# Moving a per-column scale past the down product, and summing seven block products inside three PSUM banks, in the feed-forward part of a hybrid encoder layer

## The chip, the core and the metric

The kernel runs on one core of a Trainium2 chip. Its time is the device time of one execution in microseconds (us). The core has TensorE (PE in the profile; PEld is its weight load), VectorE (DVE), ScalarE (ACT), GpSimd (POOL) and SyncE (SP), which here issues nearly all DMAs. The five engines run side by side and meet through semaphores. Matrix products end in PSUM, eight banks of 128 x 512 f32 values.

## The reference

One encoder layer for 1024 prompt positions and 32 new ones (T = 1056 columns), D = 1024, feed-forward width 4096. Two attention branches come first. What matters here is the last function:

```
h = x + m @ w_out
u = rmsnorm(h, g_ffn) @ w_up
y = h + square(relu(u)) @ w_down
```

The rmsnorm multiplies each position by r = 1/sqrt(mean(h^2) + eps). Everything is f32. As r is positive and belongs to a position, relu(r u)^2 = r^2 relu(u)^2, and r^2 can be applied after the down product too.

## The kernel before, in words

**Split products.** All matrices lie transposed: 128 features on the partitions, positions along the free dimension. An f32 operand is split into a high part and a rest (`xh`, `xl`; `wh`, `wl`), and each 128 x 128 block costs three matmuls in one PSUM chain (`three`): high by high, high by rest, rest by high. A weight unit is 128 x 512 values: a DMA into `wst` (three buffers), a cast on ACT to `wh`, a subtraction on POOL to `wl` (`unit`, `split`). `wh` and `wl` have WB = 5 buffers each, so a buffer is free again when the block that used it five units earlier has ended.

**Two groups.** Positions 0 to 511 are group one (one chunk of 512 columns), 512 to 1055 group two (two chunks of 272). In group one the feed-forward part is interleaved with the later half of attention until that ends. `go_up(f)` makes one of 32 blocks of 128 features of u (24 matmuls), `go_down(e, q)` adds to output block e of y the part of the down product that comes from up blocks 4q to 4q + 3 (12 matmuls a chunk; e and q run over 0 to 7). Group one goes up one block ahead: U0, then for each q four U and eight D (for q = 6 six D, the other two, `KEEP`, after the last three U). It has two PSUM banks, tag `pj`, for both kinds of block.

**Group two** makes two up blocks at once, for both chunks, with seven products of half the depth in place of eight (`go_up_quad`). A product is 12 matmuls of 272 columns, so a quad is 84 matmuls, and there are 16 quads. `quad_units` makes the operands on the weight side: four additions, two `sl` subtractions on DVE, two on POOL, three `wl` subtractions on POOL. On the data side they are made once, in `quarters`. Each product has a bank of its own (six banks `pj`); DVE adds them together through SBUF tiles (`part`), seven additions a quad. The down blocks use two other banks (`pd`).

**The scale.** `ffn_group` begins with a ones matmul that sums `g.acc` over the partitions, and `rsqrt` (DVE, a Sqrt on ACT, DVE). Its result `rb2` is read by every `done` of an up block: relu times r on DVE (`ru` from `pj`), square on POOL (`ru` from `ru`), cast on ACT (`xh` from `ru`), rest on DVE (`xl` from `ru`, `xh`). `go_down`'s `done` adds the bank to y, which holds h, on DVE.

**What sets the order.** Every instruction is first recorded by `Plan`, with its dependencies, a rank and a number in program order. `Plan.run` then lays out each engine's queue: whenever an engine is free in its model of durations, it takes, of the instructions that are ready, the one with the lowest (rank, number). Ranks are FAST 0 (evacuation of PSUM), PREP 1 (weights), MAIN 2 (attention), FILL 3 (the products here). The model puts some 300 ns after each instruction before another engine may use its result. The order is then fixed; on the chip each queue runs in it and waits on semaphores. As `issue` calls all of them, every row of the profile has line L408; groups are told apart by tiles.

Of the kernel before, what the change touches and what calls it, by code (L numbers as in the profile page):

```python
# [9 lines left out]
F32 = mybir.dt.float32  # L10
# [406 lines left out]
class Layer:  # L417
# [47 lines left out]
    def three(self, ps, wh, wl, xh, xl, first, last):  # L465

        mm = self.nc.tensor.matmul
        mm(ps, wh, xh, start=first, stop=False)
        mm(ps, wh, xl, start=False, stop=False)
        mm(ps, wl, xh, start=False, stop=last)  # L470
# [24 lines left out]
    def run(self):  # L495
# [32 lines left out]
        self.dg = dt([16, 128, T], "dg")  # L528

# [790 lines left out]
    def out(self, g):  # L1320

        nc, a = self.nc, self.a
        for e in (0, 4, 1, 5, 2, 6, 3, 7) if g.i else range(KB):
            units = [self.unit(a["w_out"][e, j]) for j in range(2)]

            def done(c, cs, ps, e=e):
# [4 lines left out]
                nc.vector.tensor_add(hv, ps, xr)  # L1331
                if g.i:
                    self.quarters(g, e, c, hv)
# [80 lines left out]

    def ffn_group(self, g, late=iter(())):
        nc, a, i = self.nc, self.a, g.i
        rb2 = g.acc
        for c, cs in enumerate(g.chunks):
            ps = self.bank("pj")
            nc.tensor.matmul(ps[:, :g.n], self.ones, g.acc[c], start=True, stop=True)  # L1420
            with nc.rank(FAST):
                self.rsqrt(rb2[c], ps[:, :g.n], D, lambda n: g.tmp(n, "pb", 3))
        nq, us = DFF // 512, {}

        def go_up(f):
            units = [self.unit(a["w_up"][f, j]) for j in range(2)]
            us[f] = uh, ul = g.mh[:, f % 8], g.ml[:, f % 8]

            def done(c, cs, ps):
                r = g.tmp("ru", "pb", 3)  # L1430
                nc.vector.scalar_tensor_tensor(r, ps, 0.0, rb2[c], op0=ALU.max, op1=ALU.mult)
                nc.gpsimd.tensor_mul(r, r, r)
                nc.scalar.copy(uh[:, cs], r)
                nc.vector.tensor_sub(ul[:, cs], r, uh.bitcast(F32)[:, cs])

            self.column_block(units, lambda k, cs: (g.h[:, k, cs], g.l[:, k, cs]), done, g.chunks)

        def go_up_quad(f):

            a11, a12, a22, s1, s2, s3, s4 = self.quad_units(f)  # L1440
            for i in range(2):
                us[f + i] = g.mh[:, (f + i) % 8], g.ml[:, (f + i) % 8]
            n = g.n
            ta, tb, tc, td = ([(th[:, k], tl[:, k]) for k in range(4)] for th, tl in g.sums)
            x = lambda j, c: [(g.h[:, 4 * j + k, c * n:c * n + n], g.l[:, 4 * j + k, c * n:c * n + n]) for k in range(4)]

            def product(w, xs):
                ps = self.bank("pj")[:, :n]
                with nc.rank(FILL):
                    for k in range(4):  # L1450
                        ks = slice(k * 128, k * 128 + 128)
                        self.three(ps, w[0][:, ks], w[1][:, ks], *xs[k], k == 0, k == 3)
                return ps

            z = [nc.tile(self.op, [128, 2, n], F32, "part", tag="o32", bufs=4) for _ in range(2)]
            p1, u2, u3, u4 = z[0][:, 0], z[0][:, 1], z[1][:, 0], z[1][:, 1]
            add = nc.vector.tensor_add

            def done(i, c, ps):
                cs = slice(c * n, c * n + n)  # L1460
                uh, ul = us[f + i]
                r = g.tmp("ru", "pb", 3)
                nc.vector.scalar_tensor_tensor(r, ps, 0.0, rb2[c], op0=ALU.max, op1=ALU.mult)
                nc.gpsimd.tensor_mul(r, r, r)
                nc.scalar.copy(uh[:, cs], r)
                nc.vector.tensor_sub(ul[:, cs], r, uh.bitcast(F32)[:, cs])

            ps = product(a11, x(0, 0))
            with nc.rank(FAST):
                nc.scalar.copy(p1, ps)  # L1470
            p5 = product(s1, ta)
            ps = product(s2, tb)
            with nc.rank(FAST):
                add(u2, ps, p1)
                add(u4, p5, u2)
            ps = product(a12, x(1, 0))
            with nc.rank(FAST):
                add(ps, ps, p1)
                done(0, 0, ps)
            ps = product(s3, tc)  # L1480
            with nc.rank(FAST):
                add(u3, ps, u2)
                add(ps, ps, u4)
                done(1, 1, ps)
            ps = product(s4, x(1, 1))
            with nc.rank(FAST):
                add(ps, ps, u4)
                done(0, 1, ps)
            ps = product(a22, td)
            with nc.rank(FAST):  # L1490
                add(ps, ps, u3)
                done(1, 0, ps)

        def go_down(e, q):
            units = [self.unit(a["w_down"][e, q])]

            def done(c, cs, ps):
                nc.vector.tensor_add(g.y[:, e, cs], ps, g.y[:, e, cs])
                if q == nq - 1:
                    nc.sync.dma_start(self.o["yT"][:, e, slice(g.lo + cs.start, g.lo + cs.stop)], g.y[:, e, cs])  # L1500

            self.column_block(units, lambda k, cs: (us[4 * q + k][0][:, cs], us[4 * q + k][1][:, cs]), done, g.chunks,
                              kn=4, tag="pd" if g.i else "pj")

# [13 lines left out]
        if g.i:  # L1518
            go_up_quad(0)
            go_up_quad(2)  # L1520
# [7 lines left out]
        go_up(0)  # L1528
        for q in range(nq):
# [91 lines left out]
```

## Time and profile before

| | |
|---|---|
| median of 3 runs (lowest, highest) | 1769.09 us (1766.96, 1771.07) |
| span of the profiled execution | 1767.0 us |
| time of the profiled execution outside its span | not listed |
| PE, PEld, DVE, ACT, POOL busy share | 98%, 91%, 67%, 53%, 60% |
| group one's feed-forward part | about 843 to 1296 us, attention beside it until about 1124 |
| group two's branch and output projection | about 1296 to 1391 us |
| group two's feed-forward part | 1391 us to the end |

The profile names an engine, an operation, "out<-in" by tile names, shapes, a count, then busy time and mean duration, then the engine's idle time before these instructions and what ended it. A matmul's busy time overlaps the next one's, so the pace of PE is read from starts, not from durations. In a timeline row the figures are start, duration, instruction, and in brackets the idle time before it with its releaser. In a windows row each engine has its busy time and, in brackets, its number of instructions, then the granted clock, the DMA share and GB/s.

### The profile page before, as it was taken

What the parts mean: (1) busy time and instruction counts of PE and PEld (TensorE: products, weight loads), DVE (VectorE), ACT (ScalarE), POOL (GpSimd) and SP (SyncE); (2) the same over time, 40 slices, a digit from 0 to 9 for tenths busy, and PEclk for the clock granted to TensorE, in tenths of its full rate; (3) what the DMA queues carried; (4) which work ended last, traced back from release to release, by engine and by line L of the source; (5) the groups of instructions that cost most, each with busy time, mean ns of one, the idle gap of its engine ahead of it and who ended that gap; (6) DMA issues with size and microseconds to landing.
All of it is one profiled execution on the core that took longest, in us unless ns stands there. A gap on an engine that the chain in (4) does not pass through costs nothing.

```text
span 1767.0 us, 32459 instructions
## 1 busy us (share of the span) xinstructions
PE 1739.5 (98%) x11394; PEld 1600.1 (91%) x11394; DVE 1175.5 (67%) x2427; ACT 932.7 (53%) x2007; POOL 1054.6 (60%) x901
## 2 busy tenths in 40 slices
PE   8999999999999999999999999999999999999999
PEld 7999999999899888888888888888899999999999
DVE  7555678999666645788975556333357897777764
ACT  7444598973255676766655545432236543333331
POOL 3623232435366574899875555675558986666663
PEclk9999999999999999999999999999999999999999
DMA  8244451544566668555254353433374333333312
GB/s 258 72 133 118 116 177 59 148 144 143 178 179 168 169 183 225 175 163 151 69 162 123 118 154 98 144 109 99 106 237 137 95 104 92 94 91 96 96 48 88
DMA packets 152851, 234.90 MB, mean 133 GB/s; under 512 B 27248, under 2 KB 54480, under 8 KB 152688
## 3 DMA queue, kind: packets, MB, share of 16 engines
q1 hardware_dynamic: 152256, 232.48, 45.8%
q8 instruction: 90, 1.47, 0.4%
q14 instruction: 73, 0.60, 0.1%
q10 hardware_dynamic: 432, 0.34, 0.1%
HBM read 182.58 MB, written 50.08 MB: 132 GB/s over the span
## 4 chain that ended last, share of the span: by engine, by line
PE 85%; DVE 6%; DMA 4%; POOL 3%; issue 1%; ACT 1%; SPq 0%; ACTq 0%; POOLq 0%; DVEq 0%
PE pj L408 53%; PE s L408 13%; PE pd L408 10%; PE t L408 4%; PE o L408 4%; DMA q<-dq 1%; POOL wl L408 1%; DVE xl L408 1%; DMA k<-dk 1%; DVE raw L408 1%; DVE acc L408 1%; DVE rw L408 0%; DMA o<-do 0%; SPq L408 0%; POOL acc L408 0%
## 5 line engine op out<-in xcount | busy, mean ns | idle before, releaser
L408 POOL TENSOR_TENSOR wl<-wst,wh 128x512 fp32r<-128x512 f32 x350 | 488.5, 1400 | 388.4 <-ACT wh L408 358.2
L408 PE MATMUL pj<-xh,wh 128*128 128x512 f32 (+1 forms) x1600 | 557.3, 348 | 0.6 <-DVE vt L408 0.3
L408 PE MATMUL pj<-xh,wl 128*128 128x512 f32 (+1 forms) x1600 | 557.4, 349 | 0.0
L408 PE MATMUL pj<-xl,wh 128*128 128x512 f32 (+1 forms) x1600 | 555.8, 348 | 0.0
L408 ACT CAST wh<-wst 128x512 fp32r<-128x512 f32 x350 | 216.8, 621 | 361.7 <-PE pj L408 222.0
L408 PEld LDWEIGHTS pj<-xh,wh 128*128 128x128 f32 x1600 | 301.1, 188 | 33.6 <-ACT xh L408 0.7
L408 PEld LDWEIGHTS pj<-xh,wl 128*128 128x128 f32 x1600 | 300.8, 188 | 32.7
L408 PEld LDWEIGHTS pj<-xl,wh 128*128 128x128 f32 x1600 | 301.0, 188 | 32.1
L408 PE MATMUL pd<-xh,wh 128*128 128x272 f32 x512 | 147.6, 288 | 2.0 <-DVE y L408 2.0
L408 PE MATMUL pd<-xl,wh 128*128 128x272 f32 x512 | 147.7, 288 | 0.0
L408 PE MATMUL pd<-xh,wl 128*128 128x272 f32 x512 | 147.6, 288 | 0.0
L408 DVE TENSOR_TENSOR xl<-ru,xh 128x272 fp32r<-128x272 f32 (+1 forms) x96 | 114.2, 1202 | 46.0 <-ACT xh L408 45.7
L408 DVE TENSOR_TENSOR tt<-t,tt 128x512 fp32r<-128x512 f32 (+2 forms) x168 | 100.2, 622 | 40.3 <-ACT tt L408 38.6
L408 DVE TENSOR_TENSOR_SCAN rem<-rem 128x896 f32<-128x896 f32 (+6 forms) x66 | 118.7, 1823 | 10.0 <-ACT rem L408 9.8
L408 POOL TENSOR_TENSOR p<-p,rem 128x895 f32<-128x895 f32 (+6 forms) x66 | 103.3, 1578 | 29.8 <-DVE rem L408 26.4
L408 ACT ACTIVATE junk<-score,cand 128x384 bf16<-128x384 f32 (+1 forms) x124 | 116.1, 936 | 9.3 <-DVE cand L408 7.0
L408 ACT CAST tt<-t 128x512 fp32r<-128x512 f32 (+2 forms) x168 | 84.8, 540 | 48.2 <-PE t L408 42.8
L408 DVE TENSOR_TENSOR y<-pj,y 128x512 f32<-128x512 f32 x72 | 49.6, 689 | 83.9 <-PE pj L408 83.8
L408 PE MATMUL s<-k,q 128*128 128x384 f32 (+5 forms) x384 | 95.7, 356 | 7.1 <-DMA k<-dk 2.5
L408 PE MATMUL s<-wl,xh 128*128 128x256 f32 (+1 forms) x360 | 101.8, 285 | 0.2 <-POOL wl L408 0.2
L408 PEld LDWEIGHTS o<-tt,v 128*128 128x128 f32 x640 | 93.0, 189 | 9.7 <-DVE tt L408 1.1
L408 PE MATMUL s<-wh,xh 128*128 128x256 f32 (+1 forms) x360 | 100.3, 286 | 0.9 <-DVE small L408 0.7
(245 smaller groups left out, 3963.6 us busy)
## 6 DMA issues: line engine op xcount, KB each, us to landing
wst<-w_down SPq DMA_DIRECT2D x128, 256.0 KB, 2.7
q<-dq SPq DMA_DIRECT2D x64, 256.0 KB, 5.2
wst<-w_up SPq DMA_DIRECT2D x64, 256.0 KB, 2.7
raw<-w_up SPq DMA_DIRECT2D x64, 256.0 KB, 2.8
k<-dk SPq DMA_DIRECT2D x48, 256.0 KB, 3.5
v<-dv SPq DMA_DIRECT2D x48, 256.0 KB, 3.7
wst<-w_g SPq DMA_DIRECT2D x42, 256.0 KB, 3.4
dv<-vs SPq DMA_DIRECT2D x32, 256.0 KB, 2.4
```

The costliest lines, as they stand in the source:

```text
L408: fn(*args, **kw)
```

## The change

- `rsqrt` in `ffn_group` goes; `scales` computes r^2 = 1/(mean + eps) with two DVE instructions, and is called after the first up block (group one) or the first quad (group two).
- An up block is evacuated by `square`: relu on ACT (PSUM to SBUF), r by PSUM on DVE back into PSUM, cast on ACT, rest on DVE. POOL and the scale have no part in it.
- `go_up_quad`'s products lie in chains: bank px takes a11, then s2, s3 and a22 on top; pz takes s1, then s4; py takes a12. The sums in between are copied out by ACT (`keep`), and DVE adds three times a quad instead of seven. The order of the products is a11, s1, s2, s4, a12, s3, a22.
- y no longer starts as h. For q = 0 ACT copies the bank into y; later DVE adds. Block h is stored to DRAM (`dh`) in `out` and loaded again (`hx`) once y holds q = 0 to 6; POOL then makes y r^2 + h. The last q multiplies its bank by r^2 and adds it to y, both on DVE.

```diff
         nc.vector.tensor_scalar(w, w, -0.5, 1.5, op0=ALU.mult, op1=ALU.add)
         nc.vector.tensor_mul(out, out, w)
 
-    def three(self, ps, wh, wl, xh, xl, first, last):
+    def three(self, ps, wh, wl, xh, xl, first, last, **kw):
 
         mm = self.nc.tensor.matmul
-        mm(ps, wh, xh, start=first, stop=False)
-        mm(ps, wh, xl, start=False, stop=False)
-        mm(ps, wl, xh, start=False, stop=last)
+        mm(ps, wh, xh, start=first, stop=False, **kw)
+        mm(ps, wh, xl, start=False, stop=False, **kw)
+        mm(ps, wl, xh, start=False, stop=last, **kw)
 
     def column_block(self, units, rhs, done, chunks, kn=KB, tag="pj"):
 
...
         self.dv = dt([2 * H, 128, NT, 128], "dv")
         self.do = dt([2 * H, HD, T], "do")
         self.dg = dt([16, 128, T], "dg")
+        self.dh = dt([KB, 128, T], "dh")
 
         self.wpool = nc.open("w")
         xp = nc.open("x")
...
                     nc.sync.dma_start(xr, a["xT"][:, e, slice(g.lo + cs.start, g.lo + cs.stop)])
                 hv = g.y[:, e, cs]
                 nc.vector.tensor_add(hv, ps, xr)
+                nc.sync.dma_start(self.dh[e, :, slice(g.lo + cs.start, g.lo + cs.stop)], hv)
                 if g.i:
                     self.quarters(g, e, c, hv)
                 if not g.i or c == 0 or e >= 4:
...
             p22 = part(a22, self.wpool, "w", WB, G)
         return p11, p12, p22, s1, s2, s3, s4
 
+    def square(self, g, ps, uh, ul):
+
+        nc = self.nc
+        r = g.tmp("ru", "pb", 3)
+        nc.scalar.activation(r, ps, AF.Relu)
+        nc.vector.tensor_mul(ps, ps, r)
+        nc.scalar.copy(uh, ps)
+        nc.vector.tensor_sub(ul, ps, uh.bitcast(F32))
+
     def ffn_group(self, g, late=iter(())):
         nc, a, i = self.nc, self.a, g.i
+        n = g.n
         rb2 = g.acc
-        for c, cs in enumerate(g.chunks):
-            ps = self.bank("pj")
-            nc.tensor.matmul(ps[:, :g.n], self.ones, g.acc[c], start=True, stop=True)
-            with nc.rank(FAST):
-                self.rsqrt(rb2[c], ps[:, :g.n], D, lambda n: g.tmp(n, "pb", 3))
+
+        def scales():
+
+            for c in range(len(g.chunks)):
+                ps = self.bank("pj")
+                nc.tensor.matmul(ps[:, :n], self.ones, g.acc[c], start=True, stop=True)
+                with nc.rank(FAST):
+                    v = g.tmp("rv", "pb", 3)
+                    nc.vector.tensor_scalar(v, ps[:, :n], 1.0 / D, EPS, op0=ALU.mult, op1=ALU.add)
+                    nc.vector.reciprocal(rb2[c], v)
+
         nq, us = DFF // 512, {}
 
         def go_up(f):
             units = [self.unit(a["w_up"][f, j]) for j in range(2)]
             us[f] = uh, ul = g.mh[:, f % 8], g.ml[:, f % 8]
-
-            def done(c, cs, ps):
-                r = g.tmp("ru", "pb", 3)
-                nc.vector.scalar_tensor_tensor(r, ps, 0.0, rb2[c], op0=ALU.max, op1=ALU.mult)
-                nc.gpsimd.tensor_mul(r, r, r)
-                nc.scalar.copy(uh[:, cs], r)
-                nc.vector.tensor_sub(ul[:, cs], r, uh.bitcast(F32)[:, cs])
-
-            self.column_block(units, lambda k, cs: (g.h[:, k, cs], g.l[:, k, cs]), done, g.chunks)
+            self.column_block(units, lambda k, cs: (g.h[:, k, cs], g.l[:, k, cs]),
+                              lambda c, cs, ps: self.square(g, ps, uh[:, cs], ul[:, cs]), g.chunks)
 
         def go_up_quad(f):
 
             a11, a12, a22, s1, s2, s3, s4 = self.quad_units(f)
             for i in range(2):
                 us[f + i] = g.mh[:, (f + i) % 8], g.ml[:, (f + i) % 8]
-            n = g.n
             ta, tb, tc, td = ([(th[:, k], tl[:, k]) for k in range(4)] for th, tl in g.sums)
             x = lambda j, c: [(g.h[:, 4 * j + k, c * n:c * n + n], g.l[:, 4 * j + k, c * n:c * n + n]) for k in range(4)]
 
-            def product(w, xs):
-                ps = self.bank("pj")[:, :n]
+            def product(w, xs, ps=None):
+                first = ps is None
+                if first:
+                    ps = self.bank("pj")[:, :n]
                 with nc.rank(FILL):
                     for k in range(4):
                         ks = slice(k * 128, k * 128 + 128)
-                        self.three(ps, w[0][:, ks], w[1][:, ks], *xs[k], k == 0, k == 3)
+                        self.three(ps, w[0][:, ks], w[1][:, ks], *xs[k], first and k == 0, k == 3, skip_group_check=True)
                 return ps
 
-            z = [nc.tile(self.op, [128, 2, n], F32, "part", tag="o32", bufs=4) for _ in range(2)]
-            p1, u2, u3, u4 = z[0][:, 0], z[0][:, 1], z[1][:, 0], z[1][:, 1]
-            add = nc.vector.tensor_add
-
-            def done(i, c, ps):
+            def keep(ps):
+                t = nc.tile(self.op, [128, g.w], F32, "part", tag="o32", bufs=4)[:, :n]
+                with nc.rank(FAST):
+                    nc.scalar.copy(t, ps)
+                return t
+
+            def done(i, c, out, ps, more=None):
                 cs = slice(c * n, c * n + n)
                 uh, ul = us[f + i]
-                r = g.tmp("ru", "pb", 3)
-                nc.vector.scalar_tensor_tensor(r, ps, 0.0, rb2[c], op0=ALU.max, op1=ALU.mult)
-                nc.gpsimd.tensor_mul(r, r, r)
-                nc.scalar.copy(uh[:, cs], r)
-                nc.vector.tensor_sub(ul[:, cs], r, uh.bitcast(F32)[:, cs])
-
-            ps = product(a11, x(0, 0))
-            with nc.rank(FAST):
-                nc.scalar.copy(p1, ps)
-            p5 = product(s1, ta)
-            ps = product(s2, tb)
-            with nc.rank(FAST):
-                add(u2, ps, p1)
-                add(u4, p5, u2)
-            ps = product(a12, x(1, 0))
-            with nc.rank(FAST):
-                add(ps, ps, p1)
-                done(0, 0, ps)
-            ps = product(s3, tc)
-            with nc.rank(FAST):
-                add(u3, ps, u2)
-                add(ps, ps, u4)
-                done(1, 1, ps)
-            ps = product(s4, x(1, 1))
-            with nc.rank(FAST):
-                add(ps, ps, u4)
-                done(0, 1, ps)
-            ps = product(a22, td)
-            with nc.rank(FAST):
-                add(ps, ps, u3)
-                done(1, 0, ps)
+                with nc.rank(FAST):
+                    if more is not None:
+                        nc.vector.tensor_add(out, ps, more)
+                    self.square(g, out, uh[:, cs], ul[:, cs])
+
+            px = product(a11, x(0, 0))
+            p1 = keep(px)
+            pz = product(s1, ta)
+            p5 = keep(pz)
+            product(s2, tb, px)
+            u2 = keep(px)
+            product(s4, x(1, 1), pz)
+            done(0, 1, pz, pz, u2)
+            py = product(a12, x(1, 0))
+            done(0, 0, py, py, p1)
+            product(s3, tc, px)
+            done(1, 1, self.bank("pj")[:, :n], px, p5)
+            product(a22, td, px)
+            done(1, 0, px, px)
 
         def go_down(e, q):
             units = [self.unit(a["w_down"][e, q])]
 
             def done(c, cs, ps):
-                nc.vector.tensor_add(g.y[:, e, cs], ps, g.y[:, e, cs])
-                if q == nq - 1:
-                    nc.sync.dma_start(self.o["yT"][:, e, slice(g.lo + cs.start, g.lo + cs.stop)], g.y[:, e, cs])
+                y = g.y[:, e, cs]
+                if q == 0:
+                    nc.scalar.copy(y, ps)
+                elif q < nq - 1:
+                    nc.vector.tensor_add(y, ps, y)
+                else:
+                    nc.vector.tensor_mul(ps, ps, rb2[c])
+                    nc.vector.tensor_add(y, ps, y)
+                    nc.sync.dma_start(self.o["yT"][:, e, slice(g.lo + cs.start, g.lo + cs.stop)], y)
 
             self.column_block(units, lambda k, cs: (us[4 * q + k][0][:, cs], us[4 * q + k][1][:, cs]), done, g.chunks,
                               kn=4, tag="pd" if g.i else "pj")
+            if q == nq - 2:
+                for c, cs in enumerate(g.chunks):
+                    y = g.y[:, e, cs]
+                    with nc.rank(PREP):
+                        hx = nc.tile(self.op, [128, g.w], F32, "hx", tag="sg", bufs=3)[:, :n]
+                        nc.sync.dma_start(hx, self.dh[e, :, slice(g.lo + cs.start, g.lo + cs.stop)])
+                        nc.gpsimd.tensor_mul(y, y, rb2[c])
+                        nc.gpsimd.tensor_add(y, y, hx)
 
         done = 0
 
...
 
         if g.i:
             go_up_quad(0)
+            scales()
             go_up_quad(2)
             for q in range(nq):
                 for i in range(2):
...
                         go_down(e, q)
             return
         go_up(0)
+        scales()
         for q in range(nq):
             for f in range(4 * q + 1, min(4 * q + 5, 4 * nq)):
                 go_up(f)
```

## The prediction

> **What bounds the kernel now.** First the page's head and the waits of PE from 1380 us on, then PE's pace and each engine's load by stretch.
>
> ```profile
> span 1767.0 us, 32459 instructions
> PE 1739.5 (98%) x11394; PEld 1600.1 (91%) x11394; DVE 1175.5 (67%) x2427; ACT 932.7 (53%) x2007; POOL 1054.6 (60%) x901
> ...
> PE pj L408 <- DVE ru L408: 2.3, 1, 2.3
> PE pd L408 <- DVE y L408: 2.0, 3, 0.9
> PE pj L408 <- POOL acc L408: 0.4, 2, 0.2
> ```
>
> ```profile
> 843.00:1124.00 281.00, 280.39 (x1560) 243.91 (x1560) 183.87 (x376) 153.04 (x292) 165.18 (x125) 1.00 0.42 118
> 1124.00:1296.00 172.00, 172.00 (x763) 142.51 (x762) 53.84 (x65) 54.53 (x91) 108.40 (x87) 1.00 0.43 125
> 1391.00:1480.00 89.00, 84.59 (x640) 82.46 (x639) 84.61 (x133) 38.25 (x75) 69.06 (x58) 0.98 0.29 85
> 1600.00:1700.00 100.00, 100.00 (x798) 100.00 (x797) 67.89 (x124) 36.48 (x69) 66.00 (x56) 1.00 0.30 83
> 1410.00:1413.00 3.00, 0.66 (x6) 0.44 (x5) 3.00 (x7) 0.03 (x1) 1.11 (x2) 1.00 0.31 70
> 1413.70:1417.10 3.40, 3.40 (x17) 3.40 (x16) 3.40 (x5) 2.60 (x6) 3.17 (x4) 0.50 0.35 104
> ```
>
> PE sets the time. In group two's steady part 798 matmuls take 100 us, 0.125 us each, without a gap; in group one from 1124 us it never rests either. The change leaves the number and width of these matmuls alone, so freeing POOL or DVE there is worth nothing. Only 1391 to 1480 us has something to give: PE waits 2.3 + 2.0 = 4.3 us for DVE, which is busy 84.6 of 89 us. After the 2.3 us wait the clock is granted at 0.50 for 3.4 us; 17 matmuls take 3.4 us there where the steady pace gives 2.1, another 1.3 us. At most 5.6 us can be had.
>
> The Trainium skill, "TensorE: Matmul & The Clock Gate", Part 1, says the clock halves after an idle window of about 3.4 us. By it this wait would be too short, the 1.3 us no part of the gain, and the sum below 1.3 us higher; the trace has the drop after 2.3 us, and I go by the trace.
>
> **The start of group two, part by part.** Durations by shape:
>
> ```profile
> L408 DVE TENSOR_TENSOR xl<-ru,xh 128x272 fp32r<-128x272 f32 x64 | 74.4, 1180 | 5.1 <-ACT xh L408 5.1
> L408 DVE TENSOR_TENSOR raw<-raw 128x512 f32<-128x512 f32 x64 | 56.7, 888 | 0.7 <-DMA raw<-w_up 0.3
> L408 DVE TENSOR_TENSOR pj<-pj,part 128x272 f32<-128x272 f32 x64 | 27.7, 437 | 2.8 <-PE pj L408 1.8
> L408 DVE SCALAR_TENSOR_TENSOR ru<-pj,acc 128x272 f32<-128x272 f32 x64 | 27.0, 429 | 0.5
> L408 ACT CAST xh<-ru 128x272 fp32r<-128x272 f32 x64 | 26.7, 418 | 19.2 <-POOL ru L408 19.1
> L408 POOL TENSOR_TENSOR ru<-ru 128x272 f32<-128x272 f32 x64 | 47.9, 760 | 7.3 <-DVE ru L408 7.2
> ```
>
> A quad now costs DVE seven additions (7 x 0.437), four `ru` (4 x 0.429) and four `xl` (4 x 1.18): 9.5 us, with its preparation (four `raw` additions at 0.888 and two subtractions) about 15 us, against 84 x 0.125 = 10.5 us on PE. Afterwards it is 3 additions, 4 products and 4 subtractions, each with one operand in PSUM: 11 x 0.437 = 4.8 us, with preparation about 10. The 640 matmuls of the stretch are about five quads and nine down blocks (5 x 84 + 9 x 24 = 636), so DVE loses some 23 us of its 84.6. ACT gains two copies and four relus a quad, 6 x 0.42 = 2.5 us, on 38 of 89; POOL loses 4 x 0.76 us. No evacuation waits for the scale any more. So all of the 5.6 us should be released.
>
> What is late next: a22 goes onto px straight after s3, and must wait until DVE has copied px + p5 out: 0.44 us plus about 0.25 us of matmul tail and semaphores, 0.7 us, in the first two quads, before any down block can fill in. s2 waits for ACT's copy of p1 behind one product of 1.5 us, which covers 0.42 us. Two gaps, and one more where quad two's first bank (six in the ring, two of them lent to the scale) is still being squared, filled in part: +1.0 us, bounds 0 to 4. Net **-4.6 us**, bounds -5.6 and -1.5.
>
> In the steady part down blocks are ready at every such gap, and cost nothing there; without that cover 0.7 us for each of 14 quads, 10 us.
>
> **Group one: the bank is held longer.** Two banks serve all blocks. Until now a bank of an up block was free after `ru`, one instruction; now after four, on two engines.
>
> ```profile
> L408 DVE TENSOR_TENSOR tt<-t,tt 128x512 fp32r<-128x512 f32 x100 | 66.1, 683 | 22.5 <-ACT tt L408 21.8
> L408 ACT CAST tt<-t 128x512 fp32r<-128x512 f32 x100 | 55.9, 589 | 33.6 <-PE t L408 31.9 <-ACT rem L408 0.6
> L408 DVE TENSOR_TENSOR y<-pj,y 128x512 f32<-128x512 f32 x72 | 49.6, 689 | 83.9 <-PE pj L408 83.8
> L408 DVE SCALAR_TENSOR_TENSOR ru<-pj,acc 128x512 f32<-128x512 f32 x32 | 21.9, 687 | 29.4 <-PE pj L408 29.4
> L408 ACT ACTIVATE s<-s 128x512 f32<-128x512 f32 x24 | 14.0, 583 | 15.7 <-PE s L408 14.2 <-DVE zb L408 1.5
> ```
>
> ```profile
> 1191.83 0.39 PE L408 MATMUL pj<-xh,wh 128*128 128x512 f32 x1
> ```
>
> ```profile
> 1191.85 0.62 ACT L408 CAST wh<-wst 128x512 fp32r<-128x512 f32 x1 [1.58 <-issue]
> ```
>
> ```profile
> 1192.03 0.69 DVE L408 SCALAR_TENSOR_TENSOR ru<-pj,acc 128x512 f32<-128x512 f32 x1 [0.31 <-PE pj L408]
> 1194.75 0.69 DVE L408 TENSOR_TENSOR y<-pj,y 128x512 f32<-128x512 f32 x1 [2.03 <-PE pj L408]
> ```
>
> This is the last U of a q and the first D, which starts at B = 1191.83 and lasts 2.72 us. Relu queues behind the weight cast that the same U sets free (1191.85), so it starts at about B + 0.54 and ends at B + 1.14 (`s` is a relu in PSUM, 0.583); product 0.69, copy 0.59, subtraction 0.68, some 0.05 us at each handover: free at B + 3.36. The second D wants this bank at B + 2.72: 0.65 us in which PE idles, and all that stands behind that matmul on PE moves by as much. From U to U the next block lasts twice 2.72 us, which covers it. The trains of U that end without attention as filler are four (q = 4, 5, 6 and the three before the kept blocks): **+2.6 us**, bounds 1.2 (relu before the cast) and 5.2 (the four beside attention too).
>
> The Trainium skill, "ScalarE: Activation LUTs", Rules for kernel authors, speaks against this edit: relu belongs on VectorE, up to about three times faster per element in bf16. In f32 out of PSUM the rows disagree: 0.583 on ACT, 0.687 for `ru` on DVE.
>
> **q = 6: POOL's two new instructions.** For each e (and chunk) y r^2 and + h go to POOL with the same rank as weight preparation and lower numbers than the weights five units ahead, so they win whenever ready.
>
> ```profile
> 1241.56 1.29 POOL L408 TENSOR_TENSOR wl<-wst,wh 128x512 fp32r<-128x512 f32 x1 [1.43 <-ACT wh L408]
> 1244.28 1.29 POOL L408 TENSOR_TENSOR wl<-wst,wh 128x512 fp32r<-128x512 f32 x1 [1.43 <-ACT wh L408]
> ...
> 1734.26 1.29 POOL L408 TENSOR_TENSOR wl<-wst,wh 128x512 fp32r<-128x512 f32 x1 [1.74 <-ACT wh L408]
> ```
>
> ```profile
> L408 POOL TENSOR_TENSOR acc<-acc,sq 128x272 f32<-128x272 f32 x14 | 11.7, 842 | 1.1 <-PE pj L408 1.1
> L408 POOL TENSOR_TENSOR acc<-acc,sq 128x512 f32<-128x512 f32 x7 | 11.5, 1645 | 0.2 <-ACT sq L408 0.2
> ```
>
> Group one's D at q = 6: POOL prepares one unit per 2.72 us and rests 1.43. The new pair, at the 1.29 us of a 512-wide `wl`, is 2.6. Six D in a row: the first unit goes through, then the pair of the first D, one more unit, and then ten instructions, 12.9 us, ahead of the next, ready 19 us after the first D's end. PE needs that one five buffers on, 17 us after it: 2 to 3 us of stall, I take **+2.6 us**. Bounds: 0, if weights slip in between, and 5, if the second unit misses its turn or the pair takes 1.6 (the 1.645 row) each.
>
> Group two at q = 6: two pairs a D, 4 x 0.75 = 3.0 us, per D of 3.0 us, beside a unit of 1.29 in a queue that rested 1.74. Over four D the lag is about 5 us, which the five buffers (12 us of PE) nearly absorb; the second four come out 1 us late: **+1.0 us**, bounds 0 and 5 (0.842 each, in both fours).
>
> **The rest.** The last evacuation gains a product of 0.44 us before its addition: **+0.4**. At q = 0 ACT copies instead of DVE adding, at equal length. The 24 stores of h and 24 loads go through SP's queue. A store waits for DVE's sum, a load for POOL's addition three blocks back, and weight loads queue behind both; these are fetched three buffers ahead, the DMA share is 0.29 to 0.43 in the rows above, and the nearest rows land in about 2 us, so I take 0, bounds 0 and 1:
>
> ```profile
> xr<-xT SPq DMA_DIRECT2D x16, 136.0 KB, 2.2
> out_yT<-y SPq DMA_DIRECT2D x16, 136.0 KB, 1.7
> ```
>
> **Sum.** -4.6 + 2.6 + 2.6 + 1.0 + 0.4 = +2.0 on a span of 1767.0. The median of the runs, 1769.1, is 2.1 above that span, which lies at their lower end; so 1769.1 + 2.0, **1771 us**. A measurement here can hardly tell less than 0.2%, 3.5 us, from no change, so this is "same".
>
> **Rivals.**
> - *Group one and POOL lose nothing, the start gives all* (chance 0.24): the queues' order, laid out with its 300 ns of margin, lets weights pass and U trains end better than I count. -5.6 + 1.2 + 0 + 0.4 = -4, 1765 us. For it: POOL is busy 66 of 100 us and has slack on average. Against: rank and number put the pairs first.
> - *POOL starves the weights at q = 6* (0.16): both terms at their upper bounds, 10 us in place of 3.6: +8.4, 1777.5 us, slower. It decides from 5.1 us on, 1.5 above my count. For it: the 1.645 row. Against: DVE works from PSUM at that time, and `wl` stays at 1.29.
> - *a22 waits in every quad* (0.07): +10 us, 1781 us, if the layout leaves no down block between. Against: in the steady part none is missed now.
> - *The start stays as it is* (0.05): the bank ring, not DVE, holds quad two; without the 4.6 us, 1775.7 us.
> - *Relu out of PSUM is slow on ACT* (0.02): bounded by ACT's longest row per instruction here, 1.150, it adds 0.57 us to each of the eight U trains, +4.5: 1775.7 us. For it only that row, which has twice the columns; against it the relu row of 0.583.
>
> ```profile
> L408 ACT ACTIVATE junk<-score,cand 128x1024 bf16<-128x1024 f32 x31 | 35.6, 1150 | 0.7
> ```
>
> The Trainium skill's rule named above would give an estimate of three times the 0.687 of DVE, 1.5 us a train and 1783 us in all.
>
>
> My own case has 0.46, of which 0.40 within 0.2% and 0.06 above, since its sum lies 1.5 us below that bound. Faster: 0.24. Slower: 0.06 + 0.16 + 0.07 + 0.05 + 0.02 = 0.36. The range 1764 to 1778 holds my case and the first two rivals; alone, my case has 1767 to 1773.
>
> **What would show it.** Right: no wait of PE for `ru` near 1410 us and no half clock; DVE near 60 of 89 us there; in group one PE waits of about 0.65 us for DVE's `xl` at four places between 1150 and 1275 us; one wait for POOL's `wl` of 2 to 3 us after the six D of q = 6; the last addition 0.4 us later after PE's end. Wrong: PE waits for `part` or px in every quad; none for `wl`; attention's stretch longer than 281 us.

## The result, and the profile after

The changed kernel takes 1782.84 us (median of 4 runs, 1782.26 to 1786.70) against 1768.95 us for the kernel before beside it: the ratio is 1.0083, 95% interval 1.0068 to 1.0097. It is slower, and by more than the upper end of the predicted range, 1778. The profiled execution took 1782.26 us with a span of 1780.4, 13.4 us over the span of before.

Stages are compared here between landmarks of PE: the first ones matmul, the first branch matmul of group two, the first matmul on sums (`s` tiles), the last matmul. PE's lost time is counted from the starts of its matmuls: the interval from one to the next, less the undisturbed pace, 0.1254 us (272 columns) or 0.225 us (512 columns).

| stage | before, us | after, us | difference |
|---|---|---|---|
| up to group one's feed-forward part | 843.9 | 843.6 | -0.3 |
| group one, feed-forward part | 451.3 | 462.3 | +11.0 |
| group two, branch and output | 98.9 | 98.5 | -0.4 |
| group two, feed-forward part | 369.3 | 371.9 | +2.7 |
| of it: lost in the first 90 us | 9.1 | 2.5 | -6.7 |
| of it: lost from 90 us on to 1690 us | 0.3 | 3.9 | +3.6 |
| of it: lost after 1690 us | 0.0 | 5.8 | +5.7 |
| after the last matmul | 3.6 | 4.2 | +0.5 |

First the head of the page after, and the longest waits of PE from 843 us on (total, number, longest; four rows, none above 0.7 us, are left out).

```profile
span 1780.4 us, 32518 instructions
PE 1744.9 (98%) x11394; PEld 1599.8 (90%) x11394; DVE 1107.9 (62%) x2351; ACT 978.9 (55%) x2153; POOL 1004.3 (56%) x853
...
PE pj L408 <- DVE y L408: 4.0, 5, 0.9
PE pd L408 <- POOL wl L408: 3.0, 1, 3.0
PE pj L408 <- ACT y L408: 1.8, 1, 1.8
PE pj L408 <- DVE pj L408: 1.4, 1, 1.4
PE pj L408 <- DVE xl L408: 0.8, 2, 0.6
PE pj L408 <- POOL wl L408: 0.7, 1, 0.7
```

DVE lost 67.6 us of work and POOL 50.3, and PE ended later all the same. The 2.3 us wait for DVE's `ru` is gone; eleven new waits stand in its place, in six rows, and all but the one of 1.4 us lie outside the start of group two. The table of stretches of the kernel after, with the same windows as before:

```profile
843.00:1124.00 281.00, 275.87 (x1534) 238.99 (x1533) 167.83 (x361) 160.50 (x310) 138.01 (x107) 1.00 0.42 116
1124.00:1296.00 172.00, 168.04 (x737) 137.31 (x736) 44.35 (x66) 61.34 (x104) 108.58 (x86) 1.00 0.43 123
1391.00:1480.00 89.00, 87.58 (x692) 87.08 (x692) 61.82 (x93) 53.66 (x128) 61.13 (x49) 1.00 0.39 109
1600.00:1700.00 100.00, 99.97 (x783) 98.43 (x783) 61.96 (x109) 43.26 (x95) 53.52 (x40) 1.00 0.29 85
1751.00:1754.40 3.40, 2.98 (x13) 2.98 (x14) 0.31 (x1) 0.26 (x1) 3.40 (x4) 0.50 0.31 80
```

From 1391 to 1480 us 692 matmuls fit where 640 did: 52 x 0.125 = 6.5 us gained, with DVE at 61.8 of 89 us. (Group two's part starts 10.3 us later after the change, so the window holds more of the stage ahead of it; the landmarks give 6.7.) From 1124 to 1296 us there are 737 in place of 763, at 0.225 us each 5.9 us lost. From 1600 to 1700 us there are 783 in place of 798: 15 x 0.125 = 1.9 us lost in every 100, with PE shown as 99.97% busy, so the loss is not in its idle time. After a wait of 3.0 us the clock is at 0.50 for 3.4 us near the end.

**Group one after attention.** DVE's and ACT's queues, and then PE, around one of four such places (1157, 1202, 1246 and 1281 us; timeline, start and duration in us, in brackets the idle time before and what ended it):

```profile
1199.28 0.70 DVE L408 TENSOR_TENSOR pj<-pj,ru 128x512 f32<-128x512 f32 x1 [3.40 <-ACT ru L408]
1201.04 0.69 DVE L408 TENSOR_TENSOR y<-pj,y 128x512 f32<-128x512 f32 x1 [1.05 <-PE pj L408]
1201.64 0.68 DVE L408 TENSOR_TENSOR xl<-pj,xh 128x512 fp32r<-128x512 f32 x1
```

```profile
1198.13 0.62 ACT L408 CAST wh<-wst 128x512 fp32r<-128x512 f32 x1 [2.10 <-PE pj L408]
1198.66 0.59 ACT L408 ACTIVATE ru<-pj 128x512 f32<-128x512 f32 x1
1200.02 0.59 ACT L408 CAST xh<-pj 128x512 fp32r<-128x512 f32 x1 [0.77 <-DVE pj L408]
```

```profile
1201.78 0.51 PE L408 MATMUL pj<-xh,wh 128*128 128x512 f32 x1 [0.78 <-DVE y L408]
```

Relu does stand behind the weight cast, and the four hops take the predicted 0.6 to 0.7 us each. But `xh` is ready at 1200.61, and `xl` starts only at 1201.64: ahead of it in DVE's queue is the addition to y, which waits for the down block to end. And PE's next block does not want the up block's bank at all. The order laid out gives it the other one, which the addition frees at 1201.73. So PE idles for a turn-round of the down block's own bank, 0.78 us, and the matmul starts after it run slow: 0.95 us lost at three of the places, 1.04 at the fourth, 3.9 in all. A wait for `wl` at 1267 us takes 0.90 more.

**Group one beside attention** lost another 5.6 us, where the sum counted none. The longest wait there:

```profile
893.36 3.75 DVE L408 TENSOR_TENSOR_SCAN rem<-rem 128x1024 f32<-128x1024 f32 x1 [0.24 <-ACT rem L408]
897.03 0.67 DVE L408 TENSOR_TENSOR pj<-pj,ru 128x512 f32<-128x512 f32 x1
```

```profile
897.74 0.58 ACT L408 CAST xh<-pj 128x512 fp32r<-128x512 f32 x1 [0.42 <-DVE pj L408]
898.22 0.59 ACT L408 COPY y<-pj 128x512 f32<-128x512 f32 x1
```

```profile
898.86 0.50 PE L408 MATMUL pj<-xh,wh 128*128 128x512 f32 x1 [1.77 <-ACT y L408]
```

Relu was done at 893.75. The product stood behind an attention scan of 3.75 us on DVE until 897.03, the cast behind the product, the copy of a finished down block (new at q = 0) behind the cast on ACT, and PE behind the copy: 1.97 us lost.

**Group two, first quad.** The wait of 1.4 us that is left at the start, on DVE and PE:

```profile
1412.45 1.07 DVE L408 TENSOR_TENSOR raw<-raw 128x512 f32<-128x512 f32 x1
1413.44 0.43 DVE L408 TENSOR_TENSOR pj<-pj,part 128x272 f32<-128x272 f32 x1
```

```profile
1413.93 0.40 PE L408 MATMUL pj<-xh,wh 128*128 128x272 f32 x1 [1.42 <-DVE pj L408]
```

This is a22 straight behind s3, which ended at about 1412.5. DVE had just begun a combination of up weights (`raw`) of 1.07 us, and the copy of px + p5 stands behind it. The first down block starts only at 1422, so nothing fills in.

**Group two, steady part.** DVE, POOL and PE at the one place of each 23 us period where most of the loss arises:

```profile
1663.98 1.76 DVE L408 TENSOR_TENSOR raw<-raw 128x512 f32<-128x512 f32 x1
1665.66 0.43 DVE L408 TENSOR_TENSOR pj<-pj,part 128x272 f32<-128x272 f32 x1
```

```profile
1663.89 1.30 POOL L408 TENSOR_TENSOR wl<-wst,wh 128x512 fp32r<-128x512 f32 x1 [0.93 <-ACT wh L408]
```

```profile
1665.73 0.29 PE L408 MATMUL pd<-xh,wh 128*128 128x272 f32 x1
1665.85 0.28 PE L408 MATMUL pd<-xl,wh 128*128 128x272 f32 x1
1666.15 0.39 PE L408 MATMUL pj<-xh,wh 128*128 128x272 f32 x1
```

s3 ended at about 1664.75 and a down block was there to fill in, as predicted. But DVE had just begun the last combination of up weights, and with POOL subtracting at the same time it took 1.76 us; beside no POOL work the same instruction takes 0.69. The copy of px + p5 came 0.9 us late, a little after the down block had run out. The matmul on px starts 0.30 us after the last one, though the profile shows it only 10 ns after that one's end. With the slow start that follows and a smaller one at the switch back, about 0.45 us is lost a period.

**Group two at q = 6.** Of POOL's queue, the rows around the run of pairs and one inside it, and PE's wait:

```profile
1737.53 0.77 POOL L408 TENSOR_TENSOR y<-y,acc 128x272 f32<-128x272 f32 x1 [2.74 <-DVE y L408]
1738.26 1.31 POOL L408 TENSOR_TENSOR wl<-wst,wh 128x512 fp32r<-128x512 f32 x1
1739.52 0.79 POOL L408 TENSOR_TENSOR y<-y,hx 128x272 f32<-128x272 f32 x1
...
1747.23 0.76 POOL L408 TENSOR_TENSOR y<-y,hx 128x272 f32<-128x272 f32 x1 [0.37 <-DMA hx<-dh]
...
1749.39 0.75 POOL L408 TENSOR_TENSOR y<-y,hx 128x272 f32<-128x272 f32 x1
1750.11 1.25 POOL L408 TENSOR_TENSOR wl<-wst,wh 128x512 fp32r<-128x512 f32 x1
```

```profile
1751.42 0.60 PE L408 MATMUL pd<-xh,wl 128*128 128x272 f32 x1 [2.99 <-POOL wl L408]
```

Between two weight subtractions lie 10.6 us of pairs, 0.37 of them a wait for the load of h. PE's five buffers run out, it waits 2.99 us, and the half clock after it costs some 1.4 us more; with a wait for a down bank ahead of it (0.28 us, 0.55 lost), 5.1 us.

### The profile page after: what moved, and what is told of

The parts are those of the page before. It is cut to its first block, busy times and chain, and to the rows that moved or that the text cites. A ratio compares the mean times of both kernels' runs of the same rounds, so it can differ in the third digit from the quotient of the medians.

```text
span 1780.4 us, 32518 instructions
## 1 busy us (share of the span) xinstructions
PE 1744.9 (98%) x11394; PEld 1599.8 (90%) x11394; DVE 1107.9 (62%) x2351; ACT 978.9 (55%) x2153; POOL 1004.3 (56%) x853
## 4 chain that ended last, share of the span: by engine, by line
PE 88%; DVE 4%; DMA 3%; POOL 2%; issue 1%; ACT 1%; SPq 0%; ACTq 0%; POOLq 0%; DVEq 0%
PE pj L408 55%; PE s L408 13%; PE pd L408 10%; PE t L408 5%; PE o L408 4%; DMA xt<-x 1%; POOL y L408 1%; DMA k<-dk 1%; POOL wl L408 1%; SPq L408 0%; DVE pre L408 0%; DMA o<-do 0%; DVE pen L408 0%; DMA qz<-dq 0%; DVE y L408 0%
## 5 line engine op out<-in xcount | busy, mean ns | idle before, releaser
L408 POOL TENSOR_TENSOR wl<-wst,wh 128x512 fp32r<-128x512 f32 x350 | 493.8, 1417 | 395.2 <-ACT wh L408 358.8
L408 POOL TENSOR_TENSOR p<-p,rem 128x895 f32<-128x895 f32 (+6 forms) x66 | 98.8, 1509 | 32.4 <-DVE rem L408 32.3
L408 PE MATMUL s<-wh,xl 128*128 128x256 f32 (+1 forms) x360 | 100.9, 283 | 0.0
L408 PE MATMUL o<-tt,v 128*128 128x256 f32 (+1 forms) x640 | 99.3, 278 | 1.5 <-ACT wh L408 0.8
```

What stands on the lines that cost most here:

```text
L408: fn(*args, **kw)
```

## The experiments

All are compared with the kernel before on the same chip; the changed kernel's own numbers are those above. "Lost" is PE's lost time as defined there.

**The old evacuation in group one** (relu on DVE out of PSUM, square on POOL, in SBUF; the scale stays deferred):

```diff
-            self.column_block(units, ..., lambda c, cs, ps: self.square(g, ps, uh[:, cs], ul[:, cs]), g.chunks)
+            def done(c, cs, ps):
+                r = g.tmp("ru", "pb", 3)
+                nc.vector.tensor_scalar(r, ps, 0.0, None, op0=ALU.max)
+                nc.gpsimd.tensor_mul(r, r, r)
+                nc.scalar.copy(uh[:, cs], r)
+                nc.vector.tensor_sub(ul[:, cs], r, uh.bitcast(F32)[:, cs])
+            self.column_block(units, ..., done, g.chunks)
```

> Edit to the changed kernel: in group one an up block is evacuated by one DVE relu out of PSUM into SBUF, then square on POOL, cast on ACT, rest on DVE; the scale stays behind the down product. Group two is untouched. Theory (bank hold): of the 10.9 us that group one's feed-forward part lost (451.3 to 462.3 us between its ones matmul and group two's first branch matmul), about 9 go away, because a bank is free after one instruction again: the waits of PE for y, 0.8 to 0.9 us each after each train of up blocks, and the one of 1.8 us near 897 us are gone; median near 1774 us. Rival (traffic of y and h): the loss comes from ACT's copies at q = 0, the stores of h and POOL's pairs at q = 6; then the time stays near 1783 us.

1775.52 us, ratio 1.0044 (1.0028 to 1.0060). Group one's part falls from 462.3 to 453.8 us; all waits for `y` and `xl` there are gone. Its first two stretches, 1554 and 754 matmuls against 1534 and 737:

```profile
843.00:1124.00 281.00, 278.82 (x1554) 242.99 (x1553) 172.86 (x363) 153.83 (x297) 163.55 (x126) 1.00 0.41 118
1124.00:1296.00 172.00, 170.63 (x754) 140.72 (x753) 56.39 (x69) 53.93 (x90) 128.53 (x102) 1.00 0.43 128
```

So 8.5 of the 11.0 us came with the evacuation in place, by PE's lost time 4.6 in the first stretch and 3.8 in the second. The edit frees the bank after one instruction, but it also moves relu to DVE and the square to POOL, so it does not tell the longer hold from the longer queues on ACT and DVE. POOL, with 128.5 of 172 us, now makes PE wait 1.4 us for `wl` at q = 6. A wait of 1.9 us in attention near 888 us takes more; the scale-alone run below, with the same code in group one, lacks it and takes 451.6 us there.

**POOL's pair ranked behind the weights** (SLOW is a fifth rank, behind FILL):

```diff
+                    with nc.rank(SLOW):
                         nc.gpsimd.tensor_mul(y, y, rb2[c])
                         nc.gpsimd.tensor_add(y, y, hx)
```

> Edit to the changed kernel: POOL's pair at q = 6 (y times r squared, plus h) gets the lowest rank, so weight preparation goes first. Theory (POOL starves the weights): PE's wait of 3.0 us for a weight unit near 1751 us, the half clock of 3 us after it and the 0.7 us wait near 1266 us vanish, -5 us, median near 1778 us. Rival (POOL is not the cause, the 3.0 us is a late load of h or weights): same waits, near 1783 us.

1777.93 us, ratio 1.0059 (1.0043 to 1.0075). PE has no wait of any length from 1480 us to the end, no half clock follows, and the loss after 1690 us falls from 5.8 to 0.8 us; group one is 1.8 us shorter, 0.9 of it the wait for `wl` (the runs that share the changed kernel's group one take 461.5 to 463.1 us there). POOL's queue now alternates:

```profile
1741.30 0.79 POOL L408 TENSOR_TENSOR y<-y,hx 128x272 f32<-128x272 f32 x1
1742.03 0.80 POOL L408 TENSOR_TENSOR y<-y,acc 128x272 f32<-128x272 f32 x1
1742.76 1.31 POOL L408 TENSOR_TENSOR wl<-wst,wh 128x512 fp32r<-128x512 f32 x1
```

The pairs are as many and as long as before. So it was their place in the queue that cost.

**a12 moved behind s3**, so that a product of 1.5 us covers the copy out of px:

```diff
-            py = product(a12, x(1, 0))
-            done(0, 0, py, py, p1)
             product(s3, tc, px)
             done(1, 1, self.bank("pj")[:, :n], px, p5)
+            py = product(a12, x(1, 0))
+            done(0, 0, py, py, p1)
             product(a22, td, px)
```

> Edit to the changed kernel: in a quad the product a12 (its own bank) is put between s3 and a22 (both in bank px), so that DVE's copy out of px has a product's time, 1.5 us. Theory (the chain's turn-round costs the steady part): the two slow switches per quad, together 0.46 us of PE pace per 23 us period, go, so -4 to -5 us over the steady part, median near 1778 us; the wait of 1.4 us for DVE near 1413 us goes too if it is the same turn-round. Rival (the switches wait for something else, as the down blocks' banks): no change, 1783 us.

1778.77 us, ratio 1.0059 (1.0042 to 1.0075). Lost from 1510 to 1690 us: 0.08 in place of 3.44; group two's part is 5.1 us shorter. The steady loss is the wait of a22. Whether the cover by a12 ended it is not settled here, for in this run the same combination has no POOL work beside it and takes 0.68 us. The wait of 1.4 us near the start stayed, but this edit does not test it: in the first quad PE's queue had all of a12 ahead of s3 already, and in this run too a22 stands straight behind s3.

**Seven banks again** (each product in a bank of its own, from the ring of six), with the additions on DVE as before the change, but with relu on ACT and the square in PSUM:

```diff
-            px = product(a11, x(0, 0))
-            p1 = keep(px)
...
-            product(a22, td, px)
-            done(1, 0, px, px)
+            ps = product(a11, x(0, 0))
...
+            ps = product(a22, td)
+            done(1, 0, ps, ps, u3)
```

> Edit to the changed kernel: group two's seven products again in seven banks, with the seven additions on DVE through SBUF; relu on ACT, square in PSUM and the deferred scale stay. It tells what released the start of group two (9.9 us of lost PE pace between 1350 and 1500 us before, 2.8 after). Theory (DVE's load): four more additions a quad, 1.75 us, bring back a part of it, 2 to 4 us, while the steady part loses its 0.46 us a period; both about cancel, median 1780 to 1784 us. Rival (the wait for the scale alone): the start stays as good as after the change, and the steady part gains 4 us, median near 1778 us.

1784.22 us, ratio 1.0090 (1.0073 to 1.0107). Lost in the first 90 us of group two's part: 3.8 (after 2.5, before 9.1). Lost from 1510 to 1690 us: 0.30. So the chains in three banks are worth 1.3 of the 6.7 us at the start, and give 3.1 us back in the steady part.

**The scale alone:** seven banks and, in both groups, the evacuation through SBUF (the two diffs above together, and the `done` of the first in `go_up_quad` too), so that of the change only the deferred scale with its stores, loads, copy and pairs is left.

> The kernel before with the deferred scale alone: in both groups relu on DVE out of PSUM into SBUF without the scale, square on POOL, cast on ACT, rest on DVE, seven products in seven banks; the scale, h's store and reload, ACT's copy at q = 0 and POOL's pair at q = 6 as in the change. It tells what released the start of group two (its first 90 us lost 9.1 us of PE pace before, 2.5 after the change). Theory (the wait for the scale): up blocks no longer wait for it, and 4 to 6 us come back though DVE keeps its 1.18 us rests. Rival (DVE's load, as the prediction had it): DVE still has some 15 us of work per quad against 10.5 on PE, and at most 2 us come back. Group one near its 451 us, as its banks are free after one instruction; POOL at q = 6 still costs group two about 5 us or more, since the squares come on top. Median by the theory 1770 to 1773 us, by the rival 1774 to 1777 us.

1774.93 us, ratio 1.0032 (1.0019 to 1.0045). Lost in the first 90 us of group two's part: 4.3, with DVE nearly as full as before:

```profile
1391.00:1480.00 89.00, 87.24 (x678) 85.48 (x677) 81.22 (x117) 43.57 (x94) 75.69 (x63) 1.00 0.34 101
```

DVE is busy 81.2 us here, in the kernel before 84.6, in the changed one 61.8; PE gets 678 matmuls done, against 640 and 692. So 4.8 of the 6.7 us came with the deferred scale, the rest with relu and square in place (0.5) and with the three banks (1.3), and DVE's total load was not the main thing. What of the deferred scale did it stays open. Of the 9.1 us lost before, some 4.1 lie at the wait for `ru` with its half clock, and 2.8 at the three waits for DVE's `y`. This run has none of the `y` waits at the start, for ACT empties the 16 down banks of q = 0, and DVE's work on the scale there is some 4.3 us in place of 10.6. Both are load taken off DVE just where it has no idle time (1392 to 1420 us before). Group one takes 451.6 us, as before, and the loss after 1690 us is 8.4 us: with its squares back, POOL makes PE wait 5.3 us for `wl`.

**The first three edits together:**

> The changed kernel with the three edits of the first experiments together: one-instruction release in group one, POOL's pair at the lowest rank, a12 between s3 and a22. If the three costs are separate, their gains add: 8.5 us in group one, 5.1 at q = 6, 4.1 in the steady part, 17.7 us off a span of 1780.4, 1762.7, and a median near 1765 us, faster than the kernel before by 0.2%. Rival (they share one cause, or PE loses elsewhere what it gains): 1769 us or more.

1764.20 us, ratio 0.9969 (0.9956 to 0.9981). Its lost times are those of the parts: 2.1 in the first 90 us, 0.1 in the steady part, 0.0 after 1690 us; group one takes 451.3 us.

**Group one wholly as before** (scale in its evacuation, y starting as h), group two with the change and the second and third edit:

```diff
+                    if not g.i:
+                        self.rsqrt(rb2[c], ps[:, :n], D, lambda z: g.tmp(z, "pb", 3))
+                        continue
...
+                nc.vector.scalar_tensor_tensor(r, ps, 0.0, rb2[c], op0=ALU.max, op1=ALU.mult)
...
-            if q == nq - 2:
+            if q == nq - 2 and g.i:
```

> Group one wholly as in the kernel before (scale in the up block's evacuation, h in y, no store of h); group two with the change, POOL's pair at the lowest rank and a12 between s3 and a22. Theory (all that the change has to give lies in group two's start): group one 451.3 us as before, group two's feed-forward part 362 us against 369.3 before, tail 0.5 us longer: 6.8 us less than before, median near 1762 us. Rival (group two's gain needs group one's, as the start of group two inherits its order): 1765 us or more.

1762.24 us, ratio 0.9961 (0.9948 to 0.9975), the lowest median of all, though its interval overlaps that of the three edits together. Deferring the scale gains nothing in group one (451.6 us for that part, with or without it). PE's waits from 843 us on are these:

```profile
PE pj L408 <- DVE pj L408: 1.5, 1, 1.5
PE s L408 <- DMA q<-dq: 0.8, 2, 0.4
PE pj L408 <- POOL acc L408: 0.2, 1, 0.2
```

**The last combination of up weights on POOL.** In the changed kernel with nothing else altered, so that a22 still follows s3:

```diff
-            V.tensor_sub(z, a12, z)
+            G.tensor_sub(z, a12, z)
```

> The changed kernel, but the last of a quad's four 128x512 combinations of up weights (a12 minus the sum) is done by POOL and not by DVE. In the changed kernel DVE takes it up just before product s3 ends; POOL is in a weight subtraction then, the row is 1.76 us in place of 0.69, and the copy px + p5 out of the bank that a22 wants stands behind it until 1665.66, some 0.9 us late; PE loses 0.46 us per 23 us period. Theory (the slow combination sets the lateness): with it gone from DVE the copy comes 0.9 us sooner, PE's loss from 1510 to 1690 us falls from 3.44 to 0.5 us or less, group two's FFN gets 3 to 5 us shorter (371.9 to 367-369 us), everything else as in the changed kernel: 1779 us or a little below. Rival (the turn-round of the bank by itself sets it: end of s3, copy of 0.44, semaphores): the loss stays at 3.4 us and the time at 1783. Second rival: POOL, given 1.3 us more per quad, delays weights earlier; then new waits for wl appear and the time is above 1783.

1780.45 us, ratio 1.0063 (1.0045 to 1.0080). Lost from 1510 to 1690 us: nothing (-0.1). Group two's part is 4.0 us shorter, at 368.0, though 0.9 more is lost in its first 90 us (3.4). DVE's queue at the same place of a period, where the slow combination stood:

```profile
1661.60 0.45 DVE L408 TENSOR_TENSOR pj<-pj,part 128x272 f32<-128x272 f32 x1 [0.73 <-PE pj L408]
1661.96 0.44 DVE L408 TENSOR_TENSOR pj<-pj,ru 128x272 f32<-128x272 f32 x1
1663.12 0.45 DVE L408 TENSOR_TENSOR pj<-pj,part 128x272 f32<-128x272 f32 x1 [0.72 <-PE pj L408]
```

DVE now waits 0.72 us for s3 and copies at once. So the turn-round of px by itself is hidden behind a down block, and the slow combination in front of the copy made it late.

**The same edit in the fastest version:**

> The group-two-only version (old group one, a12 after s3, POOL pair ranked last), with the same combination on POOL. Its wait near the start of group two (1.5 us for DVE's pj near 1400 us) stands among DVE instructions of 0.6 to 1.7 us on up weights. If DVE's load there is what is left, 1 us or so is to be had: 1761 us, PE's loss in the first 90 us of group two's FFN down from 2.7 to below 2. If the wait is the bank's turn-round before any down block exists, nothing changes: 1762 within 1 us. If POOL has no slack left at the start, it is slower by a wait for sl or wl.

1765.38 us, ratio 0.9980 (0.9969 to 0.9991). No gain: the wait near the start stays at 1.5 us, and the loss in the first 90 us is 3.4 in place of 2.7. There another combination of up weights, still on DVE, stands in front of the copy (1.06 us at 1404.20), and a22 again follows s3 directly. So no run has taken away what the rows show as the cause of that wait.

## Why the prediction was wrong, point by point

| term, us | predicted (bounds) | measured |
|---|---|---|
| start of group two | -4.6 (-5.6, -1.5) | -6.7 |
| bank held longer in group one | +2.6 (1.2, 5.2) | about +10 (8.5 of it taken away by the first experiment) |
| POOL at q = 6, group one | +2.6 (0, 5) | +0.9 |
| POOL at q = 6, group two | +1.0 (0, 5) | +5.1 |
| a22 in the steady part | 0 (10 as a rival) | +4.2 |
| the last evacuation | +0.4 | +0.5 |
| DMA | 0 (0, 1) | 0.37 on POOL, within the 5.1 |

The measured terms add up to +14.0; with -0.3 and -0.4 from the stages ahead, to the 13.4 us between the spans. (The 4.2 of a22 and the 5.1 of POOL are the 3.6 and 5.7 of the stage table, with what a22 costs after 1690 us put to a22.)

**Start of group two: direction right, limit and cause off.** The step that failed is the size: "at most 5.6 us can be had" added waits of 4.3 and 1.3 of half clock. The starts of the matmuls show 9.1 us lost: each wait costs 0.16 us more than its idle time and about 0.1 at the next matmul, and small waits for weight sums count too. The step "so all of the 5.6 us should be released" leaned on DVE's load falling by 23 us; the scale-alone run gave 4.8 us with DVE at 81. What was to be late next, a22 behind s3 before any down block, is late as predicted, but once (1.42 us) and not twice 0.7: a combination of 1.07 us in front of the copy was not counted. That DVE came to 61.8 us, near the forecast 60, is in part luck: the 23 us leave out the shorter work on the scale and ACT's copies, and the window holds more of the stage ahead.

**The bank in group one: the term that failed most.** Three of its assumptions fell. The second D was to want the up block's bank; the order laid out gave PE's next block the down block's own bank, behind DVE's addition. The bound of 5.2 priced every train at the bare chain of hops, 0.65 us (its hops and handovers add up to about 0.6), with only the weight cast ahead; at the four places after attention the order that `Plan` laid out put the addition to y ahead of `xl`, and each cost 0.95 to 1.04. Beside attention it assumed a filler for PE; PE had one, but DVE had too, and a 3.75 us scan stood inside the chain. Neither was read from the rows, though scans on DVE and the 300 ns that `Plan` adds per handover were both there to be read: with four hops these margins alone are 1.2 us. The first experiment shows that the evacuation in place is the cause; how the loss splits between the bare chain, the queue's order and the added work in it was read from the trace, not tested. Attention's stretch came to 281.9 us (280.0 before), one of the prediction's own signs of being wrong.

**POOL at q = 6: the rule was right, the place wrong.** Rank and number do put the pairs first, as the second experiment shows by undoing it. In group one the five buffers held better than counted, 0.9. In group two the step "the five buffers nearly absorb" failed: it took four blocks at a time, while the eight blocks of q = 6 leave one run of pairs of 10.6 us with no weight between, and the clock's drop after the wait was not in the sum. The rival "POOL starves the weights" is what happened in group two, at its upper bound of 5, and not in group one.

**The steady part: "cost nothing there" failed.** The cover was there. What was left out is the price of an instruction in front of the copy: 0.888 us is a mean over 0.68 alone and 1.1 to 1.8 beside POOL. Of the 64 combinations in the kernel before, 13 have more than 1 us of POOL work beside them and take 1.52 us in the mean, those with none 0.68; after, 27 of 64 do, at 1.65 us, and those with none take 0.69. The rival "a22 waits in every quad" is right about the place, at about 0.45 us for 0.7. The Trainium skill, "SBUF — State Buffer", Who interferes with whom, says that a DVE instruction with two SBUF operands contends with GpSimd's reads; the rows agree. Moving the combination to POOL ends the loss, but takes it out of DVE's queue altogether, so it does not test the contention by itself.

**Relu on ACT** is as cheap as the rows said, 0.596 us a 128x512 block in group one. **The rest:** the last evacuation as counted.

The errors cancelled only in part: the start and POOL in group one came out 3.8 us better than counted, but the bank, POOL in group two and a22 fell short by 15.7 us together, each priced as if its engines had little else queued.

## What to carry to other kernels

Evacuating a PSUM bank in place saves work on engines that were not the limit and lengthens the time for which the bank is taken. In group one, with two banks for all blocks, it cost 8.5 us or more; in group two, with six for the products, the same evacuation with each product in its own bank lost 0.3 us in the steady part. Where the change adds an instruction to an engine, look at what is in front of it in that queue at that moment and how long that takes beside the neighbour engine, since a mean over both cases hides it. A good change can come with a bad queue order: the same pairs, ranked last, cost nothing, and with one product moved too and group one left alone the kernel is 0.4% faster than before.

## What was not expected of the hardware

A wait that ends when the previous matmul does is not free. At nine places in the steady part PE's next matmul starts 6 to 10 ns after the modelled end of the last one, and each time 0.17 us is lost there and 0.10 at the next. Two rows of PE's weight loads, the last one before the wait and the waiting one:

```profile
1665.73 0.19 PEld L408 LDWEIGHTS pd<-xl,wh 128*128 128x128 f32 x1
1666.14 0.19 PEld L408 LDWEIGHTS pj<-xh,wh 128*128 128x128 f32 x1 [0.23 <-DVE pj L408]
```

The first starts with the matmul ahead of its own, 0.12 us early (1665.73 for the matmul of 1665.85); the second only when the wait ends, with its own matmul. That a load cannot be taken ahead past a wait is a reading of these rows. The view of waits does not list these, and PE counts as 99.97% busy.

The clock's drops last 3.413 us, or 6.827 (after the 5.3 us wait of the scale-alone run, and after a 4.0 us wait with seven banks). They went with waits of 2.3 us (before), 3.0 us (after) and, over all runs, 1.7 to 5.3 us. But a wait of 2.46 us at 673 us in the kernel before had none, nor had one of 2.87 us near 592 us in the scale-alone run. And the wait near 900 us in group one, 1.7 to 1.8 us in each run that has it, had a drop in the run with a12 moved and none in the changed kernel. So the length of the wait alone does not decide; what does was not found. The Trainium skill, "TensorE: Matmul & The Clock Gate", Part 1, gives an idle window of about 3.4 us. The drops' length agrees with it; all but the two longest of the waits that were followed by one are shorter than it.
